# Where sums run, when a norm is asked for, and where output blocks add, in a two-block transformer kernel

## The chip, the cores and the metric

One core of a Trainium2 chip runs the whole program. The time is that of one execution on the device, in microseconds (us).

## The reference

Two transformer blocks, one after the other, over 1024 tokens of 1024 features in fp32. The parts that the change meets are the two feed-forwards and, in the second block, the gates and the linear recurrent unit (LRU).

```python
# first block, its end
m = _rmsnorm(h, norm_mlp_g[l])
hid = jnp.square(jax.nn.relu(jnp.einsum('bsd,df->bsf', m, w_mlp_in[l])))
h = h + jnp.einsum('bsf,fd->bsd', hid, w_mlp_out[l])
...
# second block
q, k, v, u, y_branch, g_att, g_rec = jnp.split(z, SPLITS, axis=-1)
y_att = neighbourhood_attention(q, k, v, rpb[l]) @ w_att_o[l]
u = centred_depthwise_conv(u, conv_w[l], conv_b[l])
h_fwd = rg_lru(u, ..., False)
h_bwd = rg_lru(u, ..., True)
y_rec = ((h_fwd + h_bwd) * jax.nn.gelu(y_branch)) @ w_rec_o[l]
mixed = jax.nn.sigmoid(g_att) * y_att + jax.nn.sigmoid(g_rec) * y_rec
x = x + mixed @ w_out[l]
h2 = rms_norm(x, ln2_g[l])
x = x + jnp.square(jax.nn.relu(h2 @ w_ff1[l])) @ w_ff2[l]
```

## The kernel before

The residual stream lies in eight tiles of 128 features by 1024 tokens, and one column of 512 tokens is the width of a matmul. Each fp32 product is made of three matmuls on rounded parts, high by high, high by low and low by high. A plain job (`lin`, L439) is 8 k-steps of six matmuls. The feed-forwards use one level of Strassen's scheme instead: a step (`seven`, L1122) is twelve matmuls into one of four PSUM banks (`bk`), and seven steps per pair of quarters replace eight.

A feed-forward (`ff`) runs so. Four plain input jobs (`ff_in_job`) come first, the last two in pairs of banks, the first two in the two wide PSUM tiles (`mm`). Meanwhile a background generator (`build_t`) makes the sums of quarters of the normed activations (`ta`, `tb`, split into `tt`) that the Strassen steps need. The norm's factor `rstd` is computed in the meantime: the job before asks for it with a hook that fires after a number of k-steps (`H1`), and evacuations of the input jobs are held until it has fired. Relu takes the product times `rstd` in one DVE operation from PSUM (L1056). Then come 14 pairs of hidden tiles by seven steps each, and the output in four blocks of 28 steps (i = 1, 2, 3, 6, 7, 5, 4 by four p). For each i the operand is prepared ahead (`out_prep`): ACT rounds the high part (`obh`), DVE subtracts the low part (`obl`, L478), and POOL forms the next difference of quarters in place (L1200 to L1206). The first three blocks (`out_step`) add their seven products in accumulators `xs`; the third block mixes these into the quarters of `h` (L1241, on POOL and DVE). The last block (`block_step` with `last_ev`) adds its products straight into these quarters. The second feed-forward's last block has its own order (`end_block`).

The LRU phase runs eight groups c: two jobs (`uy_jobs`), a background front part (15 pieces, with matmuls L1766 that need ACT's sigmoids `gt`, L1753), a background back part (13 pieces) and gate jobs (`gate_job`) between. Background generators advance at each k-step (`tick`) by the job's rate, one piece in each of three lanes. After the phase come the attention output jobs, whose product times the gate is `mixed` (L1853).

All engines run their instructions in the order in which this program issues them; SP issues all loads and stores.

Of the kernel before, what the change touches and what calls it, by code (L numbers as in the profile page):

```python
# [10 lines left out]
F32 = mybir.dt.float32  # L11
# [4 lines left out]
P = 128  # L16
# [11 lines left out]
H0, H1, H2 = 22, 10, 20  # L28
# [3 lines left out]
RATE_L = (0.65, 1.0)  # L32
# [164 lines left out]
class Kern:  # L197
# [359 lines left out]

    def norm_finish(self):
        self.rstd = self.pc.tile([P, T], F32, tag="rstd", name="rstd")
        for a, ps in enumerate(self.token_sum()):  # L560
            w = self.t4(nm="nw")
            self.nc.vector.tensor_scalar(w[:, :H], ps, 1.0 / D, EPS, ALU.mult, ALU.add)
            self.rsqrt(self.rstd[:, a * H:(a + 1) * H], w)

    def norm_finish2(self, hs):

        nc = self.nc
        V = nc.vector  # L570
        v1 = self.z(nm="v1")
        for a, ps in enumerate(self.token_sum(0)):
            V.tensor_scalar(v1[:, a * H:(a + 1) * H], ps, 1.0 / D, EPS, ALU.mult, ALU.add)
        self.rstd = self.pc.tile([P, T], F32, tag="rstd", name="rstd")
        for a, ps in enumerate(self.token_sum(1)):
            sl = slice(a * H, (a + 1) * H)
            w = self.t4(nm="nw")
            V.tensor_scalar(w[:, H:], v1[:, sl], EPS, None, ALU.mult)
            V.scalar_tensor_tensor(w[:, :H], ps, 1.0 / D, w[:, H:], ALU.mult, ALU.add)
            self.rsqrt(self.rstd[:, sl], w)  # L580
        self.bg[0].append(self.keep_x1(hs, v1))
# [464 lines left out]
    def ff_in_job(self, un, i, pair, gname):  # L1046
# [26 lines left out]
    def build_t(self, gname):  # L1073

        nc = self.nc
        V, G = nc.vector, nc.gpsimd
# [3 lines left out]
        for k in range(n + 1):  # L1080
            if k < n:
# [108 lines left out]
    def out_prep(self, b, i, kk):  # L1190

        G = self.nc.gpsimd
# [25 lines left out]
    def out_step(self, un, b, p):  # L1218


        nc = self.nc
        V, G = nc.vector, nc.gpsimd
        i = un.i
        j = SEVEN_OUT.index(i)
        sl = slice((p % 2) * H, (p % 2) * H + H)

        def operand(k):
            ks = slice((k % 2) * H, (k % 2) * H + H)
            return tuple(x[:, ks] for x in self.ob[b, i, k // 2])

        def x(q):
            return self.xs[q, p // 2][:, sl]

        def alloc(q, e=None, a=None):
            if p % 2 == 0:
                self.xs[q, p // 2] = self.z(nm="xs")
            if e is not None:
                nc.sync.dma_start(x(q), half(self.res[2 * p + e], a))

        def add(eng, d, q):  # L1240
            eng.tensor_tensor(x(d), x(d), x(q), ALU.add)  # L1241

        def mix():
            if i == 2:
                add(G, 2, 1)
            elif i == 6:
                add(G, 6, 1)
                self.todo.append(lambda: self.todo.append(lambda: add(V, 3, 6)))
            elif i == 7:
                add(G, 7, 6)  # L1250
                alloc(0, 1, 1)
            elif i == 5:
                add(G, 3, 5)
                add(G, 5, 7)
            elif i == 4:
                add(G, 4, 7)
                add(V, 5, 0)
                self.h[2 * p], self.h[2 * p + 1] = [x(2), x(3)], [x(4), x(5)]

        def fn():  # L1260
            ps = self.seven(un, operand)
            todo, self.todo = self.todo, []
            for f in todo:
                f()
            for kk in AHEAD[p]:
                self.out_prep(*((b, SEVEN_OUT[j + 1]) if j < 6 else (b + 1, 1)), kk)
            self.next_loads(b + 1, i, p)
            if b == 0 and i in (1, 2, 5):
                alloc(*{1: (2, 0, 0), 2: (3, 0, 1), 5: (4, 1, 0)}[i])
            if b == 0 and i not in (2, 3, 4):  # L1270
                alloc(i)
                nc.scalar.activation(x(i), ps, AF.Copy)
            else:
                V.tensor_tensor(x(i), ps, x(i), ALU.add)  # L1274
            if b == N_BLK - 1:
                mix()
        return fn
# [972 lines left out]
```

## Time and profile before

| what | us |
|---|---|
| median of three runs | 2988.58 (2981.69 to 2990.8) |
| the profiled execution | 2983.65 |
| its span in the trace | 2981.9 |
| PE busy | 2874.7 |
| DVE busy | 1916.4 |
| ACT busy | 1170.6 |
| POOL busy | 1116.5 |

Busy times are sums over the span for each engine; the engines work beside each other. PE is busy nearly throughout, so the time follows PE's pauses, and the list of its waits and the stretches say where they are. A granted clock under 1.00 in a stretch says that PE ran part of it at the lower of its two levels, 1.2 instead of 2.4 GHz; in this trace these parts follow a pause of PE.

### The profile page before, as it was taken

The numbers are of one execution on the slowest core, as the hardware profiler recorded it, in microseconds if no ns is written. First come the engines' busy times: TensorE is split into PE (matmuls) and PEld (weight loads), VectorE is DVE, ScalarE is ACT, GpSimd is POOL, SyncE is SP. The second block draws the span as 40 slices with busy tenths as digits, with TensorE's granted clock in tenths as the row PEclk, the third lists the DMA queues.
The fourth block names the chain that finished last, engine by engine and source line by source line (L and its number), as shares of the span: only waits on it lengthen the run. The fifth ranks groups of instructions, "written<-read, shape, count | busy, mean of one in ns | idle before, by whom it ended". The sixth has DMA issues, their size and how long they took to land. (4 is left out here: it accounts for less than half of the span.)

```text
span 2981.9 us, 35224 instructions
## 1 busy us (share of the span) xinstructions
PE 2874.7 (96%) x13422; PEld 2357.2 (79%) x13422; DVE 1916.4 (64%) x2325; ACT 1170.6 (39%) x1786; POOL 1116.5 (37%) x554
## 2 busy tenths in 40 slices
PE   9999999999899999998999999998899899999987
PEld 8888787888788888876777788886788788888866
DVE  6434554666865577799743337878555855577797
ACT  3322234223354454335133325555423344444334
POOL 0020112644444443486300005455144444443486
PEclk9999999999999999999999999999999999999998
DMA  4221136776233254442423221221686233254442
GB/s 161 75 75 47 66 120 224 252 283 248 85 113 107 105 203 164 149 155 78 133 78 98 85 78 61 71 78 51 250 307 221 85 113 114 99 209 166 148 155 85
DMA packets 140056, 402.35 MB, mean 135 GB/s; under 512 B 14192, under 2 KB 32752, under 8 KB 139888
## 3 DMA queue, kind: packets, MB, share of 16 engines
q1 hardware_dynamic: 139888, 400.10, 38.5%
q8 instruction: 106, 1.74, 0.2%
q14 instruction: 62, 0.51, 0.1%
HBM read 287.75 MB, written 112.30 MB: 134 GB/s over the span
## 5 line engine op out<-in xcount | busy, mean ns | idle before, releaser
L1122 PE MATMUL bk<-obl,whi 128*128 128x512 f32 x864 | 339.3, 393 | 16.3 <-DVE obl L478 16.3
L477 ACT ACTIVATE whi<-raw 128x512 fp32r<-128x512 f32 (+2 forms) x256 | 205.1, 809 | 346.5 <-PE bk L1122 318.1
L1122 PE MATMUL bk<-obh,whi 128*128 128x512 f32 x864 | 338.0, 391 | 3.0 <-DVE xs L1334 2.0
L1122 PE MATMUL bk<-obh,wlo 128*128 128x512 f32 x864 | 338.1, 391 | 1.5 <-DVE wlo L478 1.5
L478 DVE TENSOR_TENSOR wlo<-raw,whi 128x512 fp32r<-128x512 f32 (+2 forms) x256 | 305.6, 1196 | 48.5 <-ACT whi L477 48.5
L439 PE MATMUL mm<-uh,whi 128*128 128x512 f32 x864 | 278.1, 403 | 6.7 <-DVE v L1554 5.2
L1122 PE MATMUL bk<-tt,whi 128*128 128x512 f32 x896 | 276.1, 389 | 0.2 <-DVE t L1158 0.2
L439 PE MATMUL mm<-ul,whi 128*128 128x512 f32 x864 | 269.6, 393 | 2.2 <-DVE ul L491 2.2
L378 POOL TENSOR_TENSOR wsum<-wsum 128x1024 f32<-128x1024 f32 x64 | 181.6, 2848 | 237.6 <-DMA wsum<-in_w 235.0
L439 PE MATMUL mm<-uh,wlo 128*128 128x512 f32 x864 | 267.8, 391 | 0.0
L339 DVE TENSOR_TENSOR wlo<-raw,whi 128x1024 fp32r<-128x1024 f32 (+3 forms) x140 | 221.6, 1589 | 33.9 <-ACT whi L338 33.8
L478 DVE TENSOR_TENSOR obl<-hraw,obh 128x1024 fp32r<-128x1024 f32 x112 | 196.9, 1758 | 28.5 <-ACT obh L477 25.4
L439 PEld LDWEIGHTS mm<-uh,whi 128*128 128x128 f32 x864 | 157.2, 190 | 64.7 <-issue 32.9
L1122 PEld LDWEIGHTS bk<-obl,whi 128*128 128x128 f32 x864 | 163.1, 189 | 55.1 <-DVE obl L478 21.3
L1122 PEld LDWEIGHTS bk<-tt,whi 128*128 128x128 f32 x896 | 168.1, 188 | 35.6 <-issue 0.6
L439 PEld LDWEIGHTS mm<-ul,whi 128*128 128x128 f32 x864 | 163.4, 189 | 39.0 <-DVE ul L491 4.0
L1122 PEld LDWEIGHTS bk<-obh,whi 128*128 128x128 f32 x864 | 163.1, 189 | 37.9 <-DVE xs L1334 2.4
L1122 PEld LDWEIGHTS bk<-obh,wlo 128*128 128x128 f32 x864 | 163.2, 189 | 36.2 <-DVE wlo L478 2.7
L439 PEld LDWEIGHTS mm<-uh,wlo 128*128 128x128 f32 x864 | 162.9, 189 | 35.4 <-DVE wlo L339 0.5
L338 ACT ACTIVATE whi<-raw 128x1024 fp32r<-128x1024 f32 (+3 forms) x140 | 135.6, 975 | 132.6 <-PE mm L670 63.8
L1122 PE MATMUL bk<-tt,wlo 128*128 128x512 f32 x448 | 174.3, 389 | 0.0
L1741 POOL TENSOR_SCALAR yt<-yt 128x1024 f32<-128x1024 f32 x8 | 16.8, 2100 | 411.8 <-DMA sgr<-sgr 302.7
(364 smaller groups left out, 6421.4 us busy)
## 6 DMA issues: line engine op xcount, KB each, us to landing
raw<-in_w SPq DMA_DIRECT2D x190, 512.0 KB
wsum<-in_w SPq DMA_DIRECT2D x64, 512.0 KB
sums<-wsum SPq DMA_DIRECT2D x64, 512.0 KB
hraw<-hid SPq DMA_DIRECT2D x64, 512.0 KB
raw<-sums SPq DMA_DIRECT2D x64, 512.0 KB
hid<-h SPq DMA_DIRECT2D x56, 512.0 KB
wraw<-in_w SPq DMA_DIRECT2D x28, 512.0 KB
rb<-in_rpb SPq DMA_DIRECT2D x24, 384.0 KB
```

What stands on the lines that cost most here:

```text
L338: nc.scalar.activation(un.hi, un.raw, AF.Copy)
L339: nc.vector.tensor_tensor(un.lo, un.raw, f32(un.hi), ALU.subtract)
L378: G.tensor_tensor(d, x, y, f)
L439: nc.tensor.matmul(dst[a], w, half(x, a), start=(i == 0 and q == 0), stop=(i == n - 1 and q == 2),)
L477: self.nc.scalar.activation(hi, src, AF.Copy)
L478: self.nc.vector.tensor_tensor(lo, src, f32(hi), ALU.subtract)
L1122: nc.tensor.matmul(ps, w[:, k * P:(k + 1) * P], x, start=(k == 0 and q == 0), stop=(k == n - 1 and q == 2))
L1741: G.tensor_scalar(t, t, 0.044715, 1.0, ALU.mult, ALU.add)
```

## The change

The norm is asked for three k-steps earlier (`H1` from 10 to 7: before in the second input job, now in the first). The two halves of `rstd` are computed so that both PSUM reads and ACT steps precede both Newton steps. The four input jobs all use `mm` tiles, ACT does relu without the norm's factor out of PSUM, and DVE multiplies by it afterwards. The three sums of quarters per set in `build_t` and the subtractions in `out_prep` go from POOL to DVE. All output blocks use `block_step`: the eight `h` tiles are loaded in the first steps of the first block, and every block adds into them; `out_step` and its mixing are gone. In the LRU phase all groups run at rate 0.7, the first without a gate job and the last with four; the split of the attention output (`att2_split`) starts one gate job earlier.

```diff
-H0, H1, H2 = 22, 10, 20
+H0, H1, H2 = 22, 7, 20
-RATE_L = (0.65, 1.0)
+RATE_L = 0.7
...
+    def rsqrt_halves(self, ws):
+
+        self.rstd = self.pc.tile([P, T], F32, tag="rstd", name="rstd")
+        gens = [self.rsqrt_steps(half(self.rstd, a), w, H) for a, w in enumerate(ws)]
+        for g in gens:
+            next(g)
+        for g in gens:
+            for _ in g:
+                pass
...
         def fn():
-            ps = self.lin(un, 0, self.us, pair=pair)
-            self.evac(lambda: ev(ps))
-
-        def ev(ps):
+            ps = self.lin(un, 0, self.us)
             t = self.t4(nm="relu")
-            for sl, x in self.parts(ps):
-                nc.vector.scalar_tensor_tensor(t[:, sl], x, 0.0, self.rstd[:, sl], ALU.max, ALU.mult)
+            nc.scalar.activation(t, ps, AF.Relu)
+            self.evac(lambda: ev(t))
+
+        def ev(t):
+            nc.vector.tensor_tensor(t, t, self.rstd, ALU.mult)
...
                 V.tensor_tensor(b1, b1, a1, ALU.subtract)
-                G.tensor_tensor(a1, a1, a0, ALU.subtract)
-                G.tensor_tensor(a0, a0, b1, ALU.add)
-                G.tensor_tensor(b0, b0, a0, ALU.subtract)
+                V.tensor_tensor(a1, a1, a0, ALU.subtract)
+                V.tensor_tensor(a0, a0, b1, ALU.add)
+                V.tensor_tensor(b0, b0, a0, ALU.subtract)
...
         if i == 1:
-            G.tensor_tensor(q(0, 1), q(0, 1), q(0, 0), ALU.subtract)
+            V.tensor_tensor(q(0, 1), q(0, 1), q(0, 0), ALU.subtract)
...
-    def block_step(self, un, b, p, ev, after, prep=True):
+    def block_step(self, un, b, p, ev, prep=True):
...
         def fn():
+            if (b, i) == (0, 1):
+                for m in (2 * p, 2 * p + 1):
+                    self.h_load(m, self.res)
             ps = self.seven(un, operand)
             todo, self.todo = self.todo, []
             for x in todo:
                 x()
             if prep and i != SEVEN_OUT[-1]:
                 self.prep_step(b, i, p)()
-            elif after:
-                after(p)
+            elif b < N_BLK:
+                for kk in AHEAD[p]:
+                    self.out_prep(b + 1, 1, kk)
+            if b < N_BLK:
+                self.next_loads(b + 1, i, p)
             ev(i, p, ps)
...
-                    steps.append(((un, None)[p % 2], self.out_step(Pick(un, p % 2), b, p)))
+                    steps.append(((un, None)[p % 2], self.block_step(Pick(un, p % 2), b, p, self.out_ev())))
...
-            if last:
+            if left == 1:
                 self.bg[2].append(self.att2_split())
...
-            gate_jobs(2 if c in (3, 7) else 1)
+            gate_jobs((0, 1, 1, 1, 1, 1, 1, 4)[c])
```

`out_ev` is the old `last_ev`, with the quarters taken out of whole `h` tiles: i = 1, 2, 3 and 4 are one DVE addition each from PSUM, i = 5 is two, i = 6 and 7 are one DVE addition into `uu` and one or two POOL additions into `h`; i = 1 also has an ACT copy into `uu`.

How it moves instructions, first on DVE at the first feed-forward's inputs, from the first operand set (`ta`, `tb`) on. Before:

```order
L1084 SCALAR_TENSOR_TENSOR ta<-h,cst,rstd 128x1024
L1084 SCALAR_TENSOR_TENSOR tb<-h,cst,rstd 128x1024
L1087 TENSOR_TENSOR tb<-tb,ta 128x512
L1056 SCALAR_TENSOR_TENSOR relu<-mm,rstd 128x1024 x2
L1084 SCALAR_TENSOR_TENSOR ta<-h,cst,rstd 128x1024
L1084 SCALAR_TENSOR_TENSOR tb<-h,cst,rstd 128x1024
L1087 TENSOR_TENSOR tb<-tb,ta 128x512
L478 TENSOR_TENSOR tt<-ta,tt 128x1024
L478 TENSOR_TENSOR tt<-tb,tt 128x1024
L1056 SCALAR_TENSOR_TENSOR relu<-bk,rstd 128x512 x2
```

Now, the third set on DVE and what stands behind it:

```order
L1090 SCALAR_TENSOR_TENSOR ta<-h,cst,rstd 128x1024
L1090 SCALAR_TENSOR_TENSOR tb<-h,cst,rstd 128x1024
L1093 TENSOR_TENSOR tb<-tb,ta 128x512
L1094 TENSOR_TENSOR ta<-ta 128x512
L1095 TENSOR_TENSOR ta<-ta,tb 128x512
L1096 TENSOR_TENSOR tb<-tb,ta 128x512
L1062 TENSOR_TENSOR relu<-relu,rstd 128x1024
L478 TENSOR_TENSOR wlo<-raw,whi 128x512 x4
L478 TENSOR_TENSOR tt<-ta,tt 128x1024
L478 TENSOR_TENSOR tt<-tb,tt 128x1024
```

Three sums per set (L1094 to L1096) have come onto DVE, and the relu reads SBUF, no longer a bank.

Second, on DVE in an output block (`obl` and `wlo` are low parts, `xs` and `uu` accumulators, `hraw` quarters of the hidden activations), before, in the second and third block:

```order
L478 TENSOR_TENSOR obl<-hraw,obh 128x1024
L1274 TENSOR_TENSOR xs<-bk,xs 128x512
L478 TENSOR_TENSOR wlo<-raw,whi 128x1024
L1274 TENSOR_TENSOR xs<-bk,xs 128x512
L478 TENSOR_TENSOR obl<-hraw,obh 128x1024
```

And now, in the steps of i = 6:

```order
L478 TENSOR_TENSOR obl<-hraw,obh 128x1024
L1212 TENSOR_TENSOR hraw<-hraw 128x1024
L1278 TENSOR_TENSOR uu<-bk,uu 128x512
L478 TENSOR_TENSOR wlo<-raw,whi 128x1024
L1278 TENSOR_TENSOR uu<-bk,uu 128x512
L478 TENSOR_TENSOR obl<-hraw,obh 128x1024
```

The subtraction stands between the low part and the evacuation of a bank.

Third, on PE in the last LRU group, at its gate matmuls (`bk<-uch,...`), before:

```order
L1766 MATMUL bk<-uch,rgl 128x512 x2
L439 MATMUL mm<-uh,whi 128x512 x2
L439 MATMUL mm<-ul,whi 128x512 x2
L439 MATMUL mm<-uh,wlo 128x512 x2
L1766 MATMUL bk<-uch,rgh 128x512 x2
L1766 MATMUL bk<-ucl,rgh 128x512 x2
L1766 MATMUL bk<-uch,rgl 128x512 x2
L439 MATMUL mm<-uh,whi 128x512 x2
L439 MATMUL mm<-ul,whi 128x512 x2
L439 MATMUL mm<-uh,wlo 128x512 x2
L1766 MATMUL bk<-uch,rgh 128x512 x2
```

And now:

```order
L1719 MATMUL bk<-uch,rgl 128x512 x2
L439 MATMUL mm<-uh,whi 128x512 x2
L439 MATMUL mm<-ul,whi 128x512 x2
L439 MATMUL mm<-uh,wlo 128x512 x2
L439 MATMUL mm<-uh,whi 128x512 x2
L439 MATMUL mm<-ul,whi 128x512 x2
L439 MATMUL mm<-uh,wlo 128x512 x2
L1719 MATMUL bk<-uch,rgh 128x512 x2
```

Between some of the groups two k-steps of a plain job stand now, where there was one between any two.

## Rows read from the trace of the kernel before

**Rows 1.** The page's head and the engines' busy time, share of the span and instructions.

```profile
span 2981.9 us, 35224 instructions
...
PE 2874.7 (96%) x13422; PEld 2357.2 (79%) x13422; DVE 1916.4 (64%) x2325; ACT 1170.6 (39%) x1786; POOL 1116.5 (37%) x554
```

**Rows 2.** PE's waits: total us, times, longest us, by what released them.

```profile
PE bk L1122 <- DVE relu L1056: 16.8, 2, 8.4
PE bk L1122 <- DVE obl L478: 16.3, 12, 4.7
PE bk L1766 <- ACT gt L1753: 10.9, 2, 6.6
...
PE mm L439 <- DVE mixed L1853: 5.7, 3, 3.2
...
PE mm L439 <- DVE wlo L339: 3.9, 1, 3.9
```

**Rows 3.** Busy time by stretch, (x instructions); last: PE's granted clock, DMA share, GB/s.

```profile
797.20:811.10 13.90, 5.55 (x25) 4.27 (x23) 13.83 (x10) 2.50 (x3) 11.09 (x6) 0.77 0.00 0
811.10:1077.90 266.80, 266.38 (x1165) 219.81 (x1166) 155.05 (x215) 128.37 (x210) 120.07 (x83) 0.99 0.35 124
1154.20:1230.40 76.20, 76.20 (x338) 63.10 (x337) 60.46 (x56) 28.18 (x28) 23.56 (x8) 1.00 0.46 152
1230.40:1306.60 76.20, 74.56 (x328) 61.06 (x328) 69.82 (x58) 26.41 (x26) 57.78 (x26) 1.00 0.48 159
1306.60:1391.60 85.00, 77.71 (x334) 61.84 (x332) 82.03 (x69) 36.18 (x45) 63.17 (x27) 1.00 0.25 81
2004.00:2042.00 38.00, 31.44 (x133) 25.45 (x132) 34.00 (x22) 20.56 (x24) 20.68 (x7) 0.91 0.24 81
2042.00:2080.00 38.00, 31.91 (x125) 25.00 (x124) 32.11 (x24) 17.34 (x21) 15.54 (x6) 0.91 0.14 49
2080.00:2140.00 60.00, 50.47 (x212) 40.42 (x211) 39.83 (x36) 35.17 (x37) 8.87 (x3) 0.97 0.55 206
2792.00:2868.00 76.00, 74.36 (x327) 60.94 (x326) 68.75 (x58) 28.59 (x29) 56.57 (x25) 1.00 0.50 167
2868.00:2948.00 80.00, 70.70 (x292) 56.93 (x291) 71.01 (x59) 33.88 (x42) 65.22 (x31) 0.94 0.18 60
```

**Rows 4.** Timeline of PE at the first feed-forward's inputs: start, us, instruction, [idle before].

```profile
802.36 0.39 PE L1122 MATMUL bk<-uh,wlo 128*128 128x512 f32 x1
811.14 1.19 PE L1122 MATMUL bk<-u,whi 128*128 128x512 f32 x2 [8.39 <-DVE relu L1056]
```

**Rows 5.** Timeline of DVE from the norm to the last relu there.

```profile
771.81 0.69 DVE L554 SCALAR_TENSOR_TENSOR nw<-rstd 128x512 f32<-128x512 f32 x1 [0.70 <-ACT rstd L552]
...
773.27 0.69 DVE L556 SCALAR_TENSOR_TENSOR rstd<-nw,rstd 128x512 f32<-128x512 f32 x1
...
790.27 5.49 DVE L478 TENSOR_TENSOR wlo<-raw,whi 128x512 fp32r<-128x512 f32 x4 [1.65 <-ACT whi L477]
...
801.84 1.21 DVE L478 TENSOR_TENSOR tt<-ta,tt 128x1024 fp32r<-128x1024 f32 x1
...
805.18 2.28 DVE L1084 SCALAR_TENSOR_TENSOR ta<-h,cst,rstd 128x1024 f32<-128x1024 f32 x1
...
809.70 0.69 DVE L1087 TENSOR_TENSOR tb<-tb,ta 128x512 f32<-128x512 f32 x1
810.31 1.28 DVE L1056 SCALAR_TENSOR_TENSOR relu<-bk,rstd 128x512 f32<-128x512 f32 x2
```

**Rows 6.** Timeline of POOL in the same stretch.

```profile
802.06 2.12 POOL L1088 TENSOR_TENSOR ta<-ta 128x512 f32<-128x512 f32 x1 [0.69 <-DVE tb L1087]
```

**Rows 7.** DVE's groups in the second output block: count, busy us, mean ns, idle before.

```profile
L478 DVE TENSOR_TENSOR wlo<-raw,whi 128x1024 fp32r<-128x1024 f32 x14 | 22.7, 1623 | 0.0
L478 DVE TENSOR_TENSOR obl<-hraw,obh 128x1024 fp32r<-128x1024 f32 x14 | 21.4, 1528 | 0.0
L1274 DVE TENSOR_TENSOR xs<-bk,xs 128x512 f32<-128x512 f32 x28 | 19.3, 688 | 15.7 <-PE bk L1122 15.7
```

More of the change, by code (lines that the diff above doesn't have):

```diff
@@ L556, in rsqrt_steps @@
         V.scalar_tensor_tensor(dst, t, 1.5, dst, ALU.add, ALU.mult)
+    def rsqrt_halves(self, ws):
[6 more added lines that the diff above has]
+                pass
     def norm_finish(self):
-        self.rstd = self.pc.tile([P, T], F32, tag="rstd", name="rstd")
-        for a, ps in enumerate(self.token_sum()):
-            w = self.t4(nm="nw")
+        ws = [self.t4(nm="nw") for _ in range(2)]
+        for ps, w in zip(self.token_sum(), ws):
             self.nc.vector.tensor_scalar(w[:, :H], ps, 1.0 / D, EPS, ALU.mult, ALU.add)
-            self.rsqrt(self.rstd[:, a * H:(a + 1) * H], w)
+        self.rsqrt_halves(ws)
     def norm_finish2(self, hs):
-        nc = self.nc
-        V = nc.vector
+        V = self.nc.vector
         v1 = self.z(nm="v1")
+        ws = [self.t4(nm="nw") for _ in range(2)]
         for a, ps in enumerate(self.token_sum(0)):
[L573 to L578, printed above, removed]
+            V.tensor_scalar(half(v1, a), ps, 1.0 / D, EPS, ALU.mult, ALU.add)
+            V.tensor_scalar(ws[a][:, H:], half(v1, a), EPS, None, ALU.mult)
+        for ps, w in zip(self.token_sum(1), ws):
             V.scalar_tensor_tensor(w[:, :H], ps, 1.0 / D, w[:, H:], ALU.mult, ALU.add)
-            self.rsqrt(self.rstd[:, sl], w)
+        self.rsqrt_halves(ws)
         self.bg[0].append(self.keep_x1(hs, v1))
@@ L1075, in build_t @@
         nc = self.nc
-        V, G = nc.vector, nc.gpsimd
+        V = nc.vector
         self.tt = [None] * 4
@@ L1216, in next_loads @@
             self.out_load(b, p % 2, e, (p // 2) ^ e)
[L1218 to L1277, printed above, removed]
-    def block_step(self, un, b, p, ev, after, prep=True):
+    def block_step(self, un, b, p, ev, prep=True):
         i = un.i
@@ L1309, in half_u, with out_ev @@
         return self.uu[p // 2][:, (p % 2) * H:(p % 2) * H + H]
-    def last_ev(self, after):
+    def out_ev(self, after=None):
         nc = self.nc
@@ L1317, in ev @@
             u = self.half_u(i, p)
-            (c11, c12), (c21, c22) = self.h[2 * p], self.h[2 * p + 1]
+            c11, c12, c21, c22 = (half(self.h[2 * p + e], a) for e in range(2) for a in range(2))
             if i == 1:
@@ L1336, in ev @@
                 V.tensor_tensor(c21, ps, c21, ALU.add)
-            after(i, p)
+            if after:
+                after(i, p)
         return ev
@@ L1343, in ff @@
             un = Unit(w1, 0, NC, i * P, P)
-            pr.job([un], self.ff_in_job(un, i, i in (2, 3), gname), 4 if i == N_IN0 - 1 else None)
+            pr.job([un], self.ff_in_job(un, i), 4 if i == N_IN0 - 1 else None)
         steps = []
@@ L1384, in ff @@
             return
-        ev = self.last_ev(after)
+        ev = self.out_ev(after)
         n = 28
@@ L1389, in ff @@
                 un = two[i, p // 2]
-                pr.job([un] if p % 2 == 0 else [], self.block_step(Pick(un, p % 2), N_BLK, p, ev, None),
+                pr.job([un] if p % 2 == 0 else [], self.block_step(Pick(un, p % 2), N_BLK, p, ev),
                        3 if n >= 3 else 2)
@@ L1397, in end_block @@
         self.acc, self.sqs = {}, {}
-        ev = self.last_ev(self.end_after)
+        ev = self.out_ev(self.end_after)
         later = []
@@ L1409, in end_block @@
                 pr.job(uns, self.prep_step(N_BLK, i, p), ahead)
-                later.append(self.block_step(w, N_BLK, p, ev, None, False))
+                later.append(self.block_step(w, N_BLK, p, ev, False))
                 continue
@@ L1802, in lru_back, with gate_job @@
         yield
-    def gate_job(self, un, dst, m, last=False):
+    def gate_job(self, un, dst, m, left):
         nc = self.nc
         def fn():
-            if last:
+            if left == 1:
                 self.bg[2].append(self.att2_split())
@@ L1813, in fn @@
             nc.sync.dma_start(dst[m], t)
-            if last:
+            if left == 0:
                 self.us = [None] * NC
@@ L1883, in program @@
         self.h = [None] * NC
-        self.hraw, self.ob, self.xs, self.todo = {}, {}, {}, []
+        self.hraw, self.ob, self.todo = {}, {}, []
         self.uu = {}
@@ L2016, in gate_jobs @@
                 pr.job([un := Unit("w_in_2", 0, NC, col + P * m, P)],
-                       self.gate_job(un, dst, m, not gates), ahead)
+                       self.gate_job(un, dst, m, len(gates)), ahead)
         gate_jobs(5)
@@ L2021, in program @@
         for c in range(NC):
[L2022 removed]
+            pr.rate = RATE_L
             uu = Unit("w_in_2", 0, NC, 1536 + P * c, P)
```

13 lines of the change are left out of this document (6 added, 7 removed).

## The prediction

> **What bounds the kernel now.** I read the busy shares first: PE works 2874.7 of 2981.9 us, DVE 1916 [rows 1]. The set of matmuls does not change, so only time that PE stands idle, or runs at the half clock after a pause, can be won. The list of PE's waits says where it stands, in four places. Two are the starts of the feed-forwards, where the banks wait for the DVE relu (16.8 us in 2 waits). Next come the steps of the last output block, waiting for DVE's `obl` (16.3 us in 12), then the end of the LRU phase, waiting for ACT's `gt` (10.9) and DVE's `mixed` (5.7). The `wlo` wait of 3.9 us beside these is not touched [rows 2]. Then the stretches give a ruler. The second output block runs without a pause, 338 matmuls in 76.20 us, which is 0.2254 us each; a stretch has lost its length less its matmuls times that [rows 3]. This catches the half clock too (granted 0.77, 0.91 and 0.94 there). A record or two may be missing, so a loss is good to about 0.5 us.
> - Feed-forward inputs: 13.9 us with 25 matmuls lost 8.3, the next 266.8 with 1165 lost 4.2; about 12.3 us, and as much in the other, whose relu wait is as long: 24 in all.
> - Output blocks of the first: third block 328 matmuls in 76.2, lost 2.3; fourth 334 in 85.0, lost 9.7. Of the second: 327 in 76.0, lost 2.3; and 292 in 80.0, lost 14.2. Together 28.5.
> - LRU end: 133 in 38, 125 in 38, 212 in 60: lost 8.0, 9.8 and 12.2, together 30.0, of which 3.9 is the `wlo` wait that stays: 26.1.
>
> So some 78 us are in reach; the rest of PE's waits lies in parts that are not edited.
>
> **The change part by part.**
>
> *Feed-forward inputs.* Before, PE does two steps after the four input jobs, stops at 802.36 and goes on at 811.14, when relu frees the pair banks [rows 4]. DVE is busy 13.83 of those 13.90 us [rows 3], so the wait is a queue of DVE work, running from the norm's last instruction (773.27, 0.69 us long, so 773.96) to the end of the last relu, 811.6 [rows 5]. That is 37.6 us. Four edits act on this.
>  1. The hook fires in the seventh k of the first input job instead of the second of the second job. That is three k earlier, at 10.88 us a job (48 matmuls by the ruler) / 8 = 1.36 each: 4.1 us. Both halves' ACT steps now run ahead of the Newton steps, which saves DVE's 0.70 us wait for ACT in the second half [rows 5]. `rstd` is ready 4.8 earlier, at 769.1.
>  2. Three quarter sums per operand set go to DVE: 4 sets x 3 x 0.61 us (the row at 809.70 lasts 0.69, the next starts 0.61 later [rows 5]) = 7.3 us added before the first step's evacuation. The order also has one weight split and two more `tt` splits ahead of it (three of 1.21 less 0.06 of overlap: 3.45), and I allow 2 for ACT rounds that DVE waits for. Relu by ACT and a multiply by DVE (4 x 1.13) cost DVE what its relu cost.
>  3. The sums leave POOL. While POOL adds [rows 6] a DVE operation with SBUF inputs takes 2.28 instead of 1.21 [rows 5]. Seven of the rows in the 37.6 us are such (7.5), and four weight splits took 5.49 instead of about 2.6 (2.9): 10.4. The weight sums that stay on POOL, five operations at about 0.6, keep 3. Relief: 7.4.
>  4. Relu leaves PSUM by ACT at once, so all four banks are free and PE does four steps, not two, up to 797.2 + 4 x 2.70 = 808.0.
>  DVE is through the same list at 769.1 + 37.6 + 7.3 + 3.45 + 2 - 7.4 = 812.1; the first step's evacuation stands one weight split behind, 1.2 later: 813.3. PE waits 5.3 us before the fifth step, about 1.7 before the sixth, and pays about 2 of half clock: 9.0 against 12.3, a gain of 3.3 per feed-forward, **6.6** in all. Bounds: without the relief DVE is 7.4 later and each loses 4.1 (-8 in all); with every wait hidden +24. The middle is nearest to the rows, as the relief rests on pairs of them.
>
> *Output blocks.* Mixing at the end of the third block goes (24 POOL and 8 DVE adds), and each block adds straight into `h`. DVE gets per block 8 subtracts of 128x1024 from POOL and 32 evacuations instead of 28; POOL does 12 adds of 128x512 instead of 8 subtracts. DVE work per block by whole rows: 36 operations (14 `obl`, 14 `wlo`, 8 subtracts) x 1.21 + 32 evacuations x 0.688 [rows 7] = 43.6 + 22.0 = 65.6. The second block's rows sum to 63.4 for 60.46 busy [rows 3, 7], so 0.05 of each row overlaps: 65.6 - 68 x 0.05 = 62.2. Each of the 12 POOL adds can stretch one DVE operation by 1.1 at most, so 62.2 to 75.4, say 69, of the 76.2 that PE needs. The third block now shows what such a load does: DVE 69.82, lost 2.3 [rows 3]. Evacuations stay at 0.688 there, beside POOL too, and as they now stand behind a subtract (the second pair of order rows) each comes 1.1 us later, which four banks cover. The cover would be gone if the queue slipped by more than about two steps (5.4 us). I price 0.8 lost per block for six blocks, and 1.6 for each last block, which keeps its norm work: 8. The `h` loads (8 x 512 KB from the first step of the first block) now stand in SP's queue ahead of the first weight loads and in front of evacuations that used to be ACT copies: 0 (the old `xs` were loaded in the same steps) to 3 us per feed-forward (the first addition starts at once, so one queue of loads is waited for, with four banks as cover); I take 1 each, 2. A subtract can now also hold DVE for a `hraw` load, 0 to 2 us a block, inside the 0.8. Gain: 28.5 - 8 - 2 = **18**. Bounds: all eight blocks as the third (8 x 2.3) and 6 for loads leaves 4; nothing lost, 28.
>  First the trace: evacuations, whose one input lies in PSUM, last 0.688 beside POOL, while two-SBUF-input operations double [rows 5, 7]. The Trainium skill ("GPSIMD Engine Reference", section 1, Specifications) says that GpSimd's SBUF interfaces are shared with VectorE, with contention for DVE instructions that have two SBUF inputs; by that the trace agrees, and the sum is the same.
>
> *LRU.* Rate 0.7 instead of 0.65 in the first seven groups, 0.7 instead of 1.0 in the last, which gets four gate jobs instead of two. In the last group PE asked for the gate matmuls one k apart (the third pair of order rows) and waited for ACT's sigmoid, 10.9 us in two waits [rows 2], both in the stretches from 2004 on. At 0.7 the gate matmuls stand one and two k apart, as at 0.65 in the groups before, which have no such wait. After the last front is queued there were 2 jobs x 8 k x 1.0 = 16 advances beside gate jobs, now 4 x 8 x 0.7 = 22.4, so more of the back part's ACT and DVE chain is over when the output jobs ask for `mixed`. Splitting `att2` starts one job earlier as well. Of 26.1 I take **18**: two of the waits are removed by their cause, the `mixed` ones only in part. Bounds 12 (the `mixed` waits stay, and the first group, now without a gate job, lags: 16 x 0.7 = 11.2 advances for 15 wanted) to 26.
>
> *Edits at nothing.* Newton reordering elsewhere and ACT's four relus of 128x1024 (ACT is 39% busy [rows 1]), hidden by matmuls that don't wait for them; uncovered, about as long as DVE's row of that size, 1.2 each.
>
> Sum: 6.6 + 18 + 18 = 42.6. The profiled execution took 2983.65 us, 1.8 around its span; 2983.65 - 42.6 = 2941. The median of the runs lies 4.9 above that execution, so **2946**.
>
> **Rivals.**
> 1. *DVE becomes the bound of the output blocks* (slower). For: 64 subtracts go to the engine that already ends waits there. In the fourth block DVE is busy 82.03 of 85.0 us and the block has lost 9.7. If all eight lost that, 78 stand against 28.5 now, 49 more; with the other two gains -25: 2988.6 + 25 = 3013. It decides once DVE's load with stretching passes 76.2 a block, so if the 12 adds cost over 14 us; my upper bound is 13.2. Against: the fourth block has 63 us of POOL beside it, the new ones some 20. The Trainium skill ("Perfetto Trace Analysis", Optimizing Scalar/DVE Operations) says that when DVE is saturated, offloading to Scalar or even GPSIMD may make sense, and adds that the shared port may spoil that. The first half speaks for this rival; [rows 5, 6] agree with the second. Chance 0.08.
> 2. *The wait at the inputs only moves*: DVE, with twelve more sums in its queue, frees banks as late as before or later (loss 8 instead of gain 6.6): 2946 + 15 = 2961. For: DVE is the queue that ends it. Chance 0.12.
> 3. *The LRU waits are spread, not removed*: gain 0 there, 2946 + 18 = 2964. Chance 0.10. Together with 2, or with output blocks at their bound of 4, nothing much is left: 2980 to 2990, chance 0.09.
> 4. *Nearly all goes*: 24 + 26 + 26 = 76: 2913. For: every cause is touched. Chance 0.07.
>
> **How the numbers follow.** My forecast, 2946 (2930 to 2960), has 0.54. Over 0.3%, about 9 us and what a measurement of this kernel can tell from no change, faster: 0.54 + 0.12 + 0.10 + 0.07 = 0.83; within: 0.09; slower: 0.08. The range 2924 to 2977 leaves out rival 1, most of the near-nothing case and half of rival 4, together about 0.19.
>
> **What would show it.** PE's wait on the relu gone and a wait of 4 to 7 us at the fifth step, on DVE; DVE 65 to 72 us busy in each 76 us output block, POOL 15 to 25, no long wait on `obl`; no wait on `gt` over 2 us and `mixed` waits under 4 in all. Wrong if output blocks last over 78 us, if the first group of the LRU phase shows new waits, or if PE waits for an `h` load by more than 3 us.

## The result and the profile after

The changed kernel takes 2947.5 us in the median (four runs, 2945.4 to 2949.6) against 2987.7 of the kernel before in the same sessions (2981.7 to 2990.8): a ratio of 0.9868, interval 0.985 to 0.9885. The forecast was 2946. The time came out right, but its terms did not all: by the traces the feed-forward inputs and the output blocks gave less than forecast and the LRU phase a little more. The experiments are about those terms.

The head of the page of the changed kernel, and the engines' busy time:

```profile
span 2946.6 us, 35184 instructions
...
PE 2867.4 (97%) x13422; PEld 2357.3 (80%) x13422; DVE 1920.4 (65%) x2441; ACT 1165.7 (40%) x1762; POOL 934.3 (32%) x482
```

Beside [rows 1]: PE runs the same 13422 matmuls in 7.3 us less (its mean granted clock is 0.986 instead of 0.985), POOL has lost 182 us of work, and DVE, which took over the sums and the subtractions (116 instructions more in all), is busy only 4 us longer. This last line is the surprise of the page, and the experiments come back to it.

PE's waits in the changed kernel (total us, times, longest us):

```profile
PE bk L1128 <- DVE t L1164: 17.0, 2, 8.5
...
PE bk L1128 <- DVE obl L478: 6.4, 3, 3.0
...
PE mm L439 <- DVE wlo L339: 4.2, 2, 3.9
...
PE bk L1719 <- ACT gt L1706: 3.1, 2, 2.5
PE mm L439 <- ACT uh L490: 2.6, 1, 2.6
```

Against [rows 2]: the wait at the feed-forward inputs is as long as it was (17.0 against 16.8) and has only changed its releaser, from relu to the first evacuation; `obl` fell from 16.3 to 6.4, `gt` from 10.9 to 3.1, and `mixed` has no row any more.

Stretches of the changed kernel (each engine's busy us with its instructions in brackets, in the order PE, PEld, DVE, ACT, POOL; then granted clock, DMA share, GB/s):

```profile
797.20:811.10 13.90, 11.65 (x52) 9.32 (x50) 13.82 (x10) 6.58 (x9) 9.27 (x5) 1.00 0.09 38
811.10:1077.90 266.80, 260.60 (x1139) 215.55 (x1140) 153.87 (x219) 127.83 (x210) 109.18 (x77) 0.98 0.34 122
1077.90:1154.20 76.30, 73.33 (x317) 60.22 (x316) 64.23 (x67) 32.30 (x35) 26.18 (x13) 0.98 0.65 229
1154.20:1230.40 76.20, 76.20 (x338) 63.10 (x337) 66.45 (x69) 30.19 (x32) 23.79 (x12) 1.00 0.46 152
...
1309.40:1388.60 79.20, 76.49 (x335) 62.34 (x333) 67.13 (x65) 34.36 (x36) 29.49 (x14) 1.00 0.27 87
2004.00:2042.00 38.00, 38.00 (x170) 31.45 (x169) 33.78 (x23) 21.42 (x24) 20.57 (x7) 1.00 0.20 70
2042.00:2080.00 38.00, 38.00 (x169) 31.41 (x168) 35.33 (x24) 25.90 (x30) 18.28 (x6) 1.00 0.40 143
```

They answer to [rows 3]. The two LRU stretches that had 133 and 125 matmuls are full (170 and 169). The steady output block still runs 338 matmuls in 76.20 us with DVE at 66.45, and the last block of the first feed-forward needs 79.2 us instead of 85.0. The first output block, which lost nothing before, has lost 21 matmuls (4.7 us). At the inputs, 52 matmuls instead of 25 fit in the first stretch and 1139 instead of 1165 in the next: by the ruler of 0.2254 us, 2.2 + 10.1 = 12.3 us lost, where it was 12.5.

Where the time went is clearest when the start of the n-th matmul of both traces is subtracted (both have 13422; gate jobs stand elsewhere in the LRU phase, but are as many):

| stretch, by matmul number | after minus before, us |
|---|---|
| up to the first feed-forward, 0 to 3920 | +0.7 |
| its inputs and hidden steps, to 5100 | -0.2 |
| its first output block's start, to 5160 | +4.8 |
| the rest of its output, to 6460 | -9.6 |
| start of the next block's q and k, to 6500 | +3.9 |
| to 6840 (there the norm of two halves) | -2.0 |
| attention and most of the LRU phase, to 9100 | +6.5 |
| end of the LRU phase, to 9780 | -26.5 |
| to the end of the second feed-forward's hidden steps, 12040 | 0.0 |
| its first output block's start, to 12080 | +3.8 |
| the rest of its output, to 13400 | -16.8 |

The sum is -35.4, as the spans say (2981.9 to 2946.6). The row of 0.0 hides two parts: 1.2 lost in the attention output right behind the LRU phase, and 1.2 won at the inputs of the second feed-forward. The medians are 40 apart, as the profiled execution of before took 4.1 us less than the median of its runs.

### The profile page after: what moved, and what is told of

It reads as the page before. It is cut to its first block, busy times and chain, and to the rows that moved or that the text cites. A ratio compares the mean times of both kernels' runs of the same rounds, so it can differ in the third digit from the quotient of the medians.

```text
span 2946.6 us, 35184 instructions
## 1 busy us (share of the span) xinstructions
PE 2867.4 (97%) x13422; PEld 2357.3 (80%) x13422; DVE 1920.4 (65%) x2441; ACT 1165.7 (40%) x1762; POOL 934.3 (32%) x482
## 4 chain that ended last, share of the span: by engine, by line
PE 80%; DVE 10%; ACT 3%; DMA 3%; issue 3%; SPq 1%; POOL 0%; DVEq 0%; ACTq 0%; POOLq 0%
PE bk L1128 35%; PE mm L439 32%; PE bk L1550 2%; PE bk L1584 1%; PE bk L439 1%; PE mm L674 1%; DVE wlo L339 1%; PE mm L676 1%; PE mm L675 1%; PE bk L784 1%; PE bk L1719 1%; PE bk L738 1%; PE bk L1571 1%; DMA raw<-in_w 1%; PE mm L650 1%
## 5 line engine op out<-in xcount | busy, mean ns | idle before, releaser
L439 PE MATMUL mm<-uh,whi 128*128 128x512 f32 x896 | 288.7, 404 | 10.1 <-DVE v L1507 6.0
L439 PE MATMUL mm<-ul,whi 128*128 128x512 f32 x896 | 279.9, 394 | 0.4 <-DVE ul L491 0.3
L439 PE MATMUL mm<-uh,wlo 128*128 128x512 f32 x896 | 279.1, 393 | 0.3 <-DVE wlo L339 0.3
L478 DVE TENSOR_TENSOR wlo<-raw,whi 128x512 fp32r<-128x512 f32 (+2 forms) x256 | 254.5, 997 | 38.2 <-ACT whi L477 38.2
L439 PEld LDWEIGHTS mm<-uh,whi 128*128 128x128 f32 x896 | 163.9, 190 | 69.1 <-issue 33.4
L439 PEld LDWEIGHTS mm<-ul,whi 128*128 128x128 f32 x896 | 169.8, 190 | 38.1 <-DVE ul L491 1.5
L439 PEld LDWEIGHTS mm<-uh,wlo 128*128 128x128 f32 x896 | 169.8, 190 | 37.5 <-DVE wlo L339 0.7
L1279 POOL TENSOR_TENSOR h<-h,uu 128x512 f32<-128x512 f32 x32 | 70.9, 2229 | 379.6 <-DVE uu L1278 377.9
L478 DVE TENSOR_TENSOR obl<-hraw,obh 128x1024 fp32r<-128x1024 f32 x112 | 154.7, 1381 | 13.9 <-ACT obh L477 10.8
```

The lines of the kernel that those rows point to most:

```text
L439: nc.tensor.matmul(dst[a], w, half(x, a), start=(i == 0 and q == 0), stop=(i == n - 1 and q == 2),)
L478: self.nc.vector.tensor_tensor(lo, src, f32(hi), ALU.subtract)
L1279: G.tensor_tensor(c12, c12, u, ALU.add)
```

## The experiments

Each kernel is the changed one with the edit shown (`...` stands for lines of it that are left out), and each ratio is to the kernel before on the same chip; the changed kernel's is 0.9868. A ratio is good to about 0.0015 (4.5 us), so effects of 2 to 5 us are read from the traces.

### Undoing the parts one at a time

The LRU schedule of before:

```diff
-RATE_L = 0.7
+RATE_L = (0.65, 1.0)
...
-            gate_jobs((0, 1, 1, 1, 1, 1, 1, 4)[c])
+            gate_jobs(2 if c in (3, 7) else 1)
```

> The changed kernel with the LRU schedule of before (rates 0.65 and 1.0, two gate jobs in the last group, the split of the attention output at the last gate). From the two traces, set side by side matmul by matmul, the LRU phase gained 20.0 us, so this part's own theory expects 2947.5 + 20 = 2967, with the waits on gt (10.9 us) and mixed (5.7) back and the first of the new gt waits (2.5 us) gone. A rival, that the gain there came from the shift of the earlier stages against the background work, expects under 8 us more and the waits not back.

Measured: 2965.2 us, ratio 0.9933 (0.9918 to 0.9948), 19 us slower than the changed kernel. Its waits:

```profile
PE bk L1719 <- ACT gt L1706: 12.2, 2, 6.3
...
PE mm L439 <- DVE mixed L1806: 6.1, 3, 3.2
```

Both waits of [rows 2] are back, and the `gt` wait in the middle of the phase is not among the two. The schedule's own theory holds.

The output blocks of before (`out_step`, `xs`, mixing, subtractions on POOL):

```diff
-self.block_step(Pick(un, p % 2), b, p, self.out_ev())
+self.out_step(Pick(un, p % 2), b, p)
...
-            V.tensor_tensor(q(0, 1), q(0, 1), q(0, 0), ALU.subtract)
+            G.tensor_tensor(q(0, 1), q(0, 1), q(0, 0), ALU.subtract)
...
```

> The changed kernel with the output blocks of before: accumulators and mixing, subtractions on POOL. The traces give the output blocks and the start of the next stage a gain of about 14 to 18 us (losses of 8.6 in the first blocks inside it), so this expects 2947.5 + 16 = 2963, with no wait of PE on the first addition into h, and the obl waits back (16 us in all). If the subtractions moved to DVE cost as much as the mixing did, 2948.

Measured: 2961.0, ratio 0.9917 (0.9902 to 0.9932), 15 us slower, with no wait at the first block and `obl` back:

```profile
PE bk L1128 <- DVE obl L478: 14.9, 11, 4.7
```

The feed-forward inputs of before (norm at the tenth k, pairs of banks, relu by DVE from PSUM, sums on POOL):

```diff
-H0, H1, H2 = 22, 7, 20
+H0, H1, H2 = 22, 10, 20
...
-            nc.scalar.activation(t, ps, AF.Relu)
...
+            for sl, x in self.parts(ps):
+                nc.vector.scalar_tensor_tensor(t[:, sl], x, 0.0, self.rstd[:, sl], ALU.max, ALU.mult)
...
-                V.tensor_tensor(a1, a1, a0, ALU.subtract)
...
+                G.tensor_tensor(a1, a1, a0, ALU.subtract)
...
```

> The changed kernel with the feed-forward inputs of before: pairs of banks, relu from PSUM on DVE, quarter sums on POOL, norm asked for at the tenth k. The prediction gave this part 6.6 us, so by it 2954; the traces side by side give it about 0 to 1.5 us, so by them 2948 to 2949, with one wait of about 8.4 us on relu in each feed-forward in place of one of 8.5 on the first step's evacuation.

Measured: 2943.2, ratio 0.9858 (0.9843 to 0.9872). By time that is 3 us faster than the changed kernel, inside the uncertainty; by the traces, matmul by matmul, its two feed-forward inputs are 1.0 and 1.5 us shorter than the changed kernel's (1.2 and 2.7 shorter than those of the kernel before). The wait is smaller than in either kernel:

```profile
PE bk L1128 <- DVE relu L1062: 14.0, 2, 7.0
```

The difference from the 16.8 of [rows 2], with all else at the inputs as before, is what the two halves of the norm taken together gave: 1.4 us each, the only part of the input edits that shows as a gain. The DVE timeline says the same: the norm's instructions take 5.6 us here (766.87 to 772.46) and took 7.0 (766.97 to 773.96).

### Why the wait at the inputs did not shrink

DVE's timeline in the changed kernel, from the norm to the evacuation that PE waits for (start, us, instruction, idle before in brackets):

```profile
768.80 0.69 DVE L556 SCALAR_TENSOR_TENSOR rstd<-nw,rstd 128x512 f32<-128x512 f32 x1
769.52 2.19 DVE L1090 SCALAR_TENSOR_TENSOR ta<-h,cst,rstd 128x1024 f32<-128x1024 f32 x1
...
773.67 0.69 DVE L1094 TENSOR_TENSOR ta<-ta 128x512 f32<-128x512 f32 x1
774.40 0.69 DVE L1095 TENSOR_TENSOR ta<-ta,tb 128x512 f32<-128x512 f32 x1
...
785.46 1.23 DVE L339 TENSOR_TENSOR wlo<-raw,whi 128x1024 fp32r<-128x1024 f32 x1 [2.07 <-ACT whi L338]
...
797.03 4.71 DVE L478 TENSOR_TENSOR wlo<-raw,whi 128x512 fp32r<-128x512 f32 x4 [1.64 <-ACT whi L477]
801.67 2.32 DVE L478 TENSOR_TENSOR tt<-ta,tt 128x1024 fp32r<-128x1024 f32 x1
...
814.74 1.22 DVE L1062 TENSOR_TENSOR relu<-relu,rstd 128x1024 f32<-128x1024 f32 x1
815.87 0.68 DVE L478 TENSOR_TENSOR wlo<-raw,whi 128x512 fp32r<-128x512 f32 x1
816.47 0.68 DVE L1164 TENSOR_TENSOR t<-bk,rstd 128x512 f32<-128x512 f32 x1
```

and POOL's in the same time, with PE's wait:

```profile
769.26 1.37 POOL L356 TENSOR_TENSOR wraw<-wraw 128x512 f32<-128x512 f32 x1 [31.34 <-DMA wraw<-in_w]
...
802.98 2.15 POOL L357 TENSOR_TENSOR raw<-wraw,raw 128x512 f32<-128x512 f32 x1
```

```profile
817.30 0.77 PE L1128 MATMUL bk<-uh,whi 128*128 128x512 f32 x1 [8.45 <-DVE t L1164]
```

The norm is ready at 769.5 and PE does its four steps, as forecast, but the evacuation ends at 817.2 and not at 813.3. Wherever one of POOL's six weight sums lies beside a DVE operation, that operation is about twice as long: the first `ta` (0.9 more), the four `wlo` (2.1 more) and three operations of 2.3 (3.3 more). That is 6.3 us of stretch where the sum kept 3. And each sum that needs the one before starts 0.73 after it, not 0.61, which is 1.4 on twelve.

The norm at the tenth k again:

```diff
-H0, H1, H2 = 22, 7, 20
+H0, H1, H2 = 22, 10, 20
```

> The changed kernel with the norm asked for at the tenth k again, all else as changed. If the wait before the fifth step is the end of one queue of DVE work that starts when rstd is ready, it grows from 8.5 to about 12.5 us in each feed-forward and the kernel takes 2955 to 2956. If something that does not hang on rstd ends it (a weight split, ACT), the wait stays 8.5 and the time 2947.5.

Measured: 2950.8, ratio 0.9884 (0.9867 to 0.99). The waits are 10.2 and 10.9, so the queue does hang on the norm, but 4.1 us of it are worth only 2.1 per feed-forward. DVE's timeline shows why:

```profile
765.32 1.23 DVE L339 TENSOR_TENSOR wlo<-raw,whi 128x1024 fp32r<-128x1024 f32 x1 [2.53 <-ACT whi L338]
...
772.34 1.29 DVE L1090 SCALAR_TENSOR_TENSOR ta<-h,cst,rstd 128x1024 f32<-128x1024 f32 x1
...
780.90 1.23 DVE L1062 TENSOR_TENSOR relu<-relu,rstd 128x1024 f32<-128x1024 f32 x1 [2.04 <-ACT relu L1058]
...
792.48 4.70 DVE L478 TENSOR_TENSOR wlo<-raw,whi 128x512 fp32r<-128x512 f32 x4 [1.65 <-ACT whi L477]
...
817.02 0.69 DVE L1164 TENSOR_TENSOR t<-bk,rstd 128x512 f32<-128x512 f32 x1
```

From the end of the norm to the evacuation it is 44.7 us here and 47.0 in the changed kernel. The weight split that the changed kernel does inside this queue, at 785.46 (1.15 us to the next start), is done ahead of the norm here, and the first `ta` lasts 1.29 instead of 2.19, as no weight sum of POOL lies beside it. The waits for ACT inside the queue are as long in both, 2.04 and 1.65 here, 2.07 and 1.64 there. So the earlier norm pulled other work into the queue that starts with it.

The sums back on POOL:

```diff
-                V.tensor_tensor(a1, a1, a0, ALU.subtract)
-                V.tensor_tensor(a0, a0, b1, ALU.add)
-                V.tensor_tensor(b0, b0, a0, ALU.subtract)
+                G.tensor_tensor(a1, a1, a0, ALU.subtract)
+                G.tensor_tensor(a0, a0, b1, ALU.add)
+                G.tensor_tensor(b0, b0, a0, ALU.subtract)
```

> The changed kernel with the three quarter sums of each operand set back on POOL, all else as changed. In the trace of the changed kernel DVE's queue before the first evacuation holds twelve sums at 0.62 to 0.73 us and is stretched by POOL's weight sums for only 6.4 us. If DVE work is what counts, sums on POOL take 7 to 8 us out of that queue and bring at most 4 of stretch back (10.4 in the kernel before): the wait of 8.5 falls to about 5 in each feed-forward, time 5 to 7 us under the changed kernel. If beside POOL two-input DVE operations lose as much as the sums cost, as the prediction had it (7.4 against 7.3), the wait and the time stay.

Measured: 2945.7, ratio 0.9873 (0.9858 to 0.9887), no difference in time; the waits grow to 9.4:

```profile
PE bk L1128 <- DVE t L1164: 18.8, 2, 9.4
```

So my expectation of a gain fell, and the prediction's even balance (7.3 added, 7.4 relieved) stands: twelve sums on DVE cost it about what twelve sums on POOL take from it by stretch, with 0.9 us in favour of DVE.

The six weight sums of the first two pairs on DVE:

```diff
-        G = self.nc.gpsimd
+        G = self.nc.vector if un.quad.lead else self.nc.gpsimd
...
```

> The changed kernel with the weight sums of the first two pairs (six POOL operations of 128x512 per feed-forward beside the full DVE queue) on DVE. They cost DVE 6 x 0.62 = 3.7 us and take away 6.4 us of stretch: the wait before the fifth step falls by about 2.5 us in each feed-forward, 4 to 5 us in all. If the stretch is not POOL's doing, the wait grows by 3.7 instead.

Measured: 2940.1, ratio 0.9852 (0.9837 to 0.9867); the waits fall by 2.2 each, as expected. Its DVE timeline has six operations more before the same evacuation, and reaches it 3.5 us earlier (812.97), of which 1.25 is only that this run was so much ahead at the inputs already:

```profile
PE bk L1129 <- DVE t L1165: 12.5, 2, 6.3
```

```profile
801.39 1.22 DVE L479 TENSOR_TENSOR tt<-ta,tt 128x1024 fp32r<-128x1024 f32 x1
...
803.66 1.28 DVE L1091 SCALAR_TENSOR_TENSOR ta<-h,cst,rstd 128x1024 f32<-128x1024 f32 x1
...
812.97 0.68 DVE L1165 TENSOR_TENSOR t<-bk,rstd 128x512 f32<-128x512 f32 x1
```

The operations that lasted 2.3 last 1.22 and 1.28 here. The stretch is POOL's doing.

Relu as before, by DVE out of pairs of banks, with sums on DVE and the early norm kept:

```diff
-            ps = self.lin(un, 0, self.us)
-            nc.scalar.activation(t, ps, AF.Relu)
+            ps = self.lin(un, 0, self.us, pair=pair)
...
```

> The changed kernel with only relu as before (by DVE from PSUM with the norm's factor, the last two jobs in pairs of banks); sums on DVE and the early norm kept. The last relu now stands behind all four operand sets and six splits on DVE, so it ends at about 814.5; PE has done two steps, not four, and goes on then, so the fifth step comes at about 820 against 817.3: 2 to 3 us slower in each feed-forward, 5 in all, if the freed banks give what the prediction put on them. If relu's place does not matter because the queue's end decides, the time stays.

Measured: 2952.8, ratio 0.989 (0.9872 to 0.9908). PE stops two steps earlier and waits 12.3 in each:

```profile
PE bk L1128 <- DVE relu L1062: 24.6, 2, 12.3
```

By the traces, matmul by matmul, the two feed-forwards are 3.2 and 4.4 us slower, more than the 2 to 3 expected, so the freed banks do give what was put on them. Each of the three edits, undone alone, makes the inputs slower by the traces (the norm by 2.2 and 2.5 us, the sums by 1.0 and 1.4); all three undone together make them faster. The order in the old arrangement suggests how that can be: with the norm three k later, the generator's pieces come three k later in DVE's order as well. In the kernel with the old inputs the last relu stands directly behind the fourth set's first sum and frees PE at 809.7. In this last kernel two more `tt` splits and three sums stand in front of it, and it frees PE at 814.4.

```profile
808.22 0.69 DVE L1093 TENSOR_TENSOR tb<-tb,ta 128x512 f32<-128x512 f32 x1
808.83 1.28 DVE L1062 SCALAR_TENSOR_TENSOR relu<-bk,rstd 128x512 f32<-128x512 f32 x2
...
815.18 0.68 DVE L1164 TENSOR_TENSOR t<-bk,rstd 128x512 f32<-128x512 f32 x1
```

These rows are of the kernel with the old inputs; it reaches the first evacuation at 815.18, 1.3 ahead of the changed kernel (0.8 of it is that this run was ahead already), although its norm comes 3 us later. That the order of the pieces alone is worth this was not tried.

### The first output block

In the changed kernel DVE stands still in front of the second addition into `h`, and PE behind it:

```profile
1089.30 0.69 DVE L1274 TENSOR_TENSOR h<-bk,h 128x512 f32<-128x512 f32 x1 [4.14 <-DMA h<-res]
1089.90 1.22 DVE L478 TENSOR_TENSOR obl<-hraw,obh 128x1024 fp32r<-128x1024 f32 x1
```

```profile
1091.17 0.50 PE L1128 MATMUL bk<-obl,whi 128*128 128x512 f32 x1 [2.97 <-DVE obl L478]
```

PE's wait is put down to `obl`, but `obl` was only next in the queue. The loads of `h` in the last two input steps instead:

```diff
-            if (b, i) == (0, 1):
-                for m in (2 * p, 2 * p + 1):
-                    self.h_load(m, self.res)
...
+                4: [(self.h_load, (m, self.res)) for m in range(4)],
+                3: [(self.out_prep, (0, 1, 1))] + [(self.h_load, (m, self.res)) for m in range(4, NC)]}
```

> The changed kernel with the eight loads of h put out in the last two input steps, ahead of the last store of the hidden activations, instead of in the first output steps. If the two waits of PE for obl (3.0 and 2.5 us), with their half clock, are DVE's queue standing behind an addition that waits for h to land, both go and the time is 7 to 9 us less than the changed kernel's. If the wait is for room or for another load, they stay.

Measured: 2937.0, ratio 0.9844 (0.9829 to 0.9859), 7 us faster than the changed kernel; both waits are gone and the first block is whole:

```profile
1077.90:1154.20 76.30, 76.30 (x338) 63.22 (x337) 67.23 (x70) 32.19 (x35) 27.26 (x13) 1.00 0.63 231
```

### The LRU phase

A new wait stands in the middle of the phase:

```profile
1891.54 0.79 PE L1719 MATMUL bk<-uch,rgh 128*128 128x512 f32 x1 [2.51 <-ACT gt L1706]
```

One gate job in the first group, three in the last:

```diff
-            gate_jobs((0, 1, 1, 1, 1, 1, 1, 4)[c])
+            gate_jobs((1, 1, 1, 1, 1, 1, 1, 3)[c])
```

> The changed kernel with a gate job again in the first LRU group and three in the last instead of none and four. If the new wait for gt in the middle of the phase (2.5 us and a half clock, 5.7 us in all) comes from the background lagging since the first group, it goes; the last group has 16.8 advances after its last front instead of 22.4, so a gt or mixed wait of 2 to 4 us may come back at the end: 2 to 5 us faster than the changed kernel. If the lag is not the cause the wait stays and the kernel is slower by what comes back at the end.

Measured: 2946.8, ratio 0.9876 (0.986 to 0.9893): the time stays. The middle wait is gone (7.1 us with its half clock, by the starts of matmuls 8800 to 9100), and `mixed` has come back at the end:

```profile
PE mm L439 <- DVE mixed L1806: 6.1, 2, 3.3
```

The first half of the trade is as told. The second is not: the end of the phase gives back 9.7 us (waits of 3.3 and 2.8, and half clock behind them), where I had allowed 2 to 4, so the LRU phase as a whole is 2.6 us slower than the changed kernel's.

### The subtractions

```diff
-            V.tensor_tensor(q(0, 1), q(0, 1), q(0, 0), ALU.subtract)
+            G.tensor_tensor(q(0, 1), q(0, 1), q(0, 0), ALU.subtract)
...
```

> The changed kernel with the subtractions of the output operands back on POOL (64 of 128x1024), accumulation straight into h kept. Per block DVE gives up 8 x 1.13 = 9.0 us and gets the stretch back that the second block of the kernel before shows (36 us of split operations at 1.21 took 44.1 there: about 10). Steady blocks of the changed kernel have DVE at 66.5 of 76.2 us and no wait, so by that view nothing changes there, and only the last blocks, where POOL also has the norm's sums, lose 2 to 8 us in all: 2948 to 2955. If DVE's load were near the bound that slows the blocks, taking 9 us off it would make the kernel faster than the changed one by over 2 us.

Measured: 2958.1, ratio 0.9907 (0.989 to 0.9925), about 11 us slower than the changed kernel and more than I had expected. With eight subtractions fewer per block DVE is busier than with them, 70.42 us against 66.45 in the same stretch:

```profile
1154.20:1230.40 76.20, 76.20 (x338) 63.15 (x337) 70.42 (x61) 30.23 (x33) 50.03 (x21) 1.00 0.45 152
```

```profile
L478 DVE TENSOR_TENSOR wlo<-raw,whi 128x1024 fp32r<-128x1024 f32 x15 | 29.7, 1980 | 0.5 <-ACT whi L477 0.5
```

The weight splits take 1.98 us in the mean there. In the changed kernel the same group reads

```profile
L478 DVE TENSOR_TENSOR wlo<-raw,whi 128x1024 fp32r<-128x1024 f32 x14 | 18.0, 1284 | 0.5 <-ACT whi L477 0.5
```

This block shows DVE's load, but it is not where the time goes: PE runs its 338 matmuls in 76.20 us with either. Matmul by matmul, the loss against the changed kernel lies in the first blocks (2.1 us with `obl` waits of 3.2 and 1.6, and 2.4 us with waits of 3.2 and 1.4) and in the last block of the second feed-forward (4.2 us, with an `obl` wait of 1.9 and half clock behind it).

### What beats both

The two edits that helped, together (weight sums of the first pairs on DVE, early loads of `h`):

> Two edits together on the changed kernel: the weight sums of the first two pairs on DVE (alone: 0.9852 of the kernel before) and the loads of h in the last input steps (alone: 0.9844). They act in different places, so if both causes are as told their gains add: 5 + 8 to 10 us under the changed kernel, a ratio of about 0.982, 2932.

Measured: 2930.2, ratio 0.9818 (0.9802 to 0.9834), as their sum. With a gate job moved from ahead of the phase into its first group as well:

```diff
-        gate_jobs(5)
+        gate_jobs(4)
...
-            gate_jobs((0, 1, 1, 1, 1, 1, 1, 4)[c])
+            gate_jobs((1, 1, 1, 1, 1, 1, 1, 4)[c])
```

> The same two edits, and one gate job taken from ahead of the LRU phase into its first group, so that the first group has one and the last still four. If the gt wait in the middle (2.5 us, 5.5 with its half clock) comes from the lag of the first group and the mixed waits at the end from too few gate jobs in the last, both are gone and this is 4 to 6 us faster than the two edits alone: 2927. If the gate job is missed ahead of the phase, where it covers the attention's background work, a new wait there takes that back.

Measured: 2930.7, ratio 0.9822 (0.9806 to 0.9837). The middle wait is gone, but a `mixed` wait of 3.4 us is there in spite of the four gate jobs:

```profile
PE mm L440 <- DVE mixed L1807: 3.4, 1, 3.4
```

So the number of gate jobs in the last group is not all that decides that wait. By the traces the phase up to its last group is 5.5 us shorter than with the two edits alone, and the end 6.2 longer. In both kernels that add a gate job to the first group of the new schedule the middle wait goes and a `mixed` wait comes at the end. So the wait may only move, as it would if the background's chain sets the end of the phase; what decides it was not settled.

## Why the prediction was right, and which of its steps were not

**Feed-forward inputs: 6.6 forecast, about 1.4 by the traces.** Here rival 2 came true in its cause, though not in its loss: the wait moved and kept its length. The order of events was right (norm at 769.5 for 769.1, four steps of PE instead of two, the first evacuation as the releaser). The term that was mis-sized is the stretch that the weight sums left on POOL would keep, 3 us for 6.3; I had given five operations 0.6 each, while rows of the kernel before already showed a 128x1024 operation at 2.28 beside one such sum [rows 5, 6]. The 0.61 per sum was taken from a row whose successor did not depend on it; in a chain it is 0.73. The experiments bear out the stretch of the weight sums, the even balance of the other sums, and the freed banks. The three k of the earlier norm were priced in full, 4.1, and are worth 2.1, as a weight split and a stretched `ta` come into the queue with them. The gain of 1.4 (0.2 in the first feed-forward, 1.2 in the second) is less than the joined halves of the norm give by themselves (1.4 each, priced at 0.7), so the other input edits together won nothing. A slip beside this: the two losses before, 8.3 and 4.2, add up to 12.5 and not 12.3, which would have made the forecast for this part 7.0.

**Output blocks: 18 forecast, 14 to 18 measured** (15 by time, 17.8 by the traces, less 3.9 at the start of the next stage). The parts cancelled. The loads of `h` were priced at 1 us each, with 3 as their bound, and cost 4.8 and 3.8: DVE works in order, so the addition that waited held the next operand's low part too, and the four banks that I named as cover protect PE's results and not its operands. The steady blocks were priced at 0.8 each and lose nothing, with DVE at 66.45 where I had said 69. The subtractions, which I had counted as a load on DVE (rival 1 rested on them), are worth some 11 us on that engine, in the first and last blocks. Not in the sum at all was the start of the next stage: PE waits 2.55 us for an operand `uh`, which is made in one piece of 128x1024, where it was made in halves. A second cause is as near: the addition into `h` that `uh` needs stands on DVE behind a weight split of 3.41 us, nearly three times the 1.23 of the row at 785.46.

```profile
1398.14 3.41 DVE L339 TENSOR_TENSOR wlo<-raw,whi 128x1024 fp32r<-128x1024 f32 x1
```

Neither was tried apart, and the same place costs between 1.6 and 4.0 us in the runs that share this code.

**LRU: 18 forecast, 20 by the traces, 19 by the experiment.** The end gave 26.5, nearly the 26.1 that could be had, and the first group's lag, which I had named as a bound, cost some 6 in the middle. Whether those 6 can be had is open, as both kernels that removed the wait paid as much or more at the end. I had said that a lag would show as waits in the first group; it shows several groups later, at 1891.

**Rival 1** needed twelve POOL additions to cost DVE over 14 us a block. Against the 62.2 of the prediction they cost 66.45 - 62.2 = 4.3. **Rivals 3 and 4** did not happen.

**Signs.** DVE at 66.45 and POOL at 23.79 us a block are as told. The wait at the fifth step is 8.5 and not 4 to 7, one `gt` wait is 2.5 where none was to be over 2, and the first output blocks last about 81 us, over the 78 that I had called a sign of being wrong.

**The sum.** By the traces the three parts gave 1.4 + 13.9 + 20.0 = 35.3 and not 42.6: the first two 5.2 and 4.1 less than forecast, the third 2.0 more. Newton's steps elsewhere, put at nothing, stand in a stretch that became 2.0 shorter, about as much as other stretches lost. So the closeness of the forecast is in part luck. For the profiled execution the sum said 2941, and it took 2948.4. The medians lie 40.2 apart because the profiled execution of before was 4.1 under its median and that of the changed kernel 0.8 above.

## What to carry to other kernels

Before work is moved off a busy VectorE to GpSimd, or back, add up what each GpSimd operation does to the VectorE operations out of SBUF that run beside it: here work moved onto the busier engine made that engine less busy. When an accumulator is loaded ahead of its first addition, the load belongs ahead of the queue that holds the addition, since everything behind it in order waits too. A queue that starts earlier need not end earlier by as much: look at which other work comes into it with the earlier start, as the weight split did here.

## What the runs showed of the hardware

The stretch goes both ways. The 128x1024 split `tt` goes from 1.22 to 2.31 us beside a POOL addition of 128x512, and that addition goes from 1.29 to 2.15, while the evacuations, with one input in PSUM, stay at 0.68. It is not confined to operations with two inputs: in the LRU phase of the changed kernel `zu<-zu,cst`, which reads one tensor, in SBUF, lasts 0.75 us alone and twice that beside POOL.

```profile
841.00 1.29 POOL L357 TENSOR_TENSOR raw<-wraw,raw 128x512 f32<-128x512 f32 x1 [3.16 <-issue]
...
1759.42 0.75 DVE L1678 TENSOR_SCALAR zu<-zu,cst 128x1024 f32<-128x1024 f32 x1
...
1828.94 4.31 POOL L1731 TENSOR_SCALAR th<-th 128x1024 f32<-128x1024 f32 x1
1829.98 1.52 DVE L1678 TENSOR_SCALAR zu<-zu,cst 128x1024 f32<-128x1024 f32 x1
```

I had not expected that 9 us of work added to DVE per block would lower its busy time by 4.
